# A hybrid decoder layer on one core: both matmuls of the MLP as 2x2 Strassen products, in two stages

## The chip, the core and the metric

The kernel runs on one core of a Trainium2 chip. The metric is the device time of one execution in microseconds; the time before is the median of three runs. Engine names follow the profile: PE (TensorE), DVE (VectorE), ACT (ScalarE), POOL (GpSimd), SP (SyncE, which issues nearly all transfers).

## What is computed

One layer over x of shape (1, 1024, 1024) float32. Three token mixers (an mLSTM, a short convolution, stick-breaking attention) come out of one input projection, are projected, gated and summed, and go through an output projection into the residual. The change touches only what follows:

```
x = x + merged @ w_out[l]                                   # 1024 x 1024
h2 = rmsnorm(x, norm_mlp_g[l])
x = x + jnp.square(jax.nn.relu(h2 @ w_up[l])) @ w_down[l]   # 1024 x 4096, 4096 x 1024
return rmsnorm(x, norm_final_g)
```

## The kernel before

**Arithmetic.** Each operand of a dense matmul is kept as two float32r tiles: `hi`, a copy made by ACT, and `lo`, the remainder made by DVE (`split`, lines 134 to 140). `mm3` (129 to 132) multiplies them with three matmuls: hi by hi, hi by lo, lo by hi. Every 128x128 by 128x512 product is thus three PE instructions.

**Storage.** Buffers lie in rings that are handed out and given back in program order: `ring_r` 64 tiles (names gr) of float32r operands, `ring_f` 23 float32 tiles (gf), `ring_wr` two raw weight tiles of 1056 columns (wr), `ring_wh` and `ring_wl` five each for the halves of a weight (wh, wl), and eight PSUM banks of 128x512 (ps). A buffer is written again only when its last reader is done.

**Order.** The program is traced in the order of the source; a scheduler then orders each engine's instructions by its own estimate of the times, and each engine runs its list in that order.

**Output projection and second norm** (740 to 808). For each of 8 tiles of 128 tokens, two groups of 24 matmuls make the product with `w_out`; DVE adds the residual (773), ACT squares with a sum (776), POOL takes the power -0.5 (204). After four tiles the normed tokens are multiplied by gain and factor (794), transposed on PE (800) and split straight from PSUM into `h2`, 8 x 2 pairs of 128x512.

**MLP** (810 to 848). Eight blocks F of 512 hidden columns. For each of 4 hidden tiles of a block, `dense_ws` (159) loads 1024x128 of `w_up`, splits it, and makes two groups of 24 matmuls, one per half of the tokens; ACT applies the Relu (822), DVE squares (823) and the result is split into `gT`. `load_rows` brings 128 rows of `w_down`. Then 16 groups of 12 matmuls (841) make the block's contribution for 8 token tiles by 2 halves of the columns, and DVE adds each to the residual `x1` (842), which stays in SBUF.

**End** (850 to 866). For each token tile two Squares, the factor, two multiplications (865) and two stores.

Of the kernel before, what the change touches and what calls it, by code (L numbers as in the profile page):

```python
# [38 lines left out]
def hybrid_block_kernel(  # L39
# [27 lines left out]
    # rings of equal buffers, handed out and given back in program order  # L67
# [74 lines left out]
    def load_split(src, k, parts):  # L142
        """Loads k rows of weights per partition and splits them into the (hi, lo) parts."""
# [557 lines left out]
    # branch projections under their gates  # L701
# [38 lines left out]
    # output projection, residual, second norm  # L740
# [12 lines left out]
    gb = [ring_f.get() for _ in range(2)]  # L753
    for c in range(2):
        nc.sync.dma_start(gb[c][:, :512], norm_mlp_g[:, c * 512:(c + 1) * 512].broadcast_to([P, 512]))
    x1 = [None] * 8
    rss = [None] * 8
    h2 = [[None, None] for _ in range(KO)]
    for th in range(2):
        for tl in range(4):  # L760
            tt = th * 4 + tl
            sl = slice(tl * P, (tl + 1) * P)
# [21 lines left out]
        if th == 1:
            for w2 in wo:
                free_all([w2])
        for ko in range(KO):
            h2[ko][th] = (g("mh"), g("mh"))
        for c in range(2):
            for t2 in range(2):  # L790
                xn = [ring_f.get(), ring_f.get()]
                for ti in range(2):
                    tt = th * 4 + t2 * 2 + ti
                    nc.vector.scalar_tensor_tensor(xn[ti][:, :512], x1[tt][c][:, :512], rss[tt], gb[c][:, :512], ALU.mult, ALU.mult)
# [99 lines left out]
```

## Time and profile before

| what | value |
|---|---|
| median of 3 runs | 2579.2 us (2579.11 to 2579.5) |
| span of the profiled execution | 2577.4 us, 1.8 us below that median |
| PE | busy 99% of the span, 13176 matmuls |
| DVE, ACT, POOL | busy 50%, 36%, 14% |
| granted PE clock | 0.999 of full speed |
| moved by DMA | 156.4 MB, 61 GB/s on average |

The profiled execution has no run time of its own beside its span; the span goes from its first to its last instruction. A matmul's "busy" time overlaps with the next one's, so the distance from one to the next is had by dividing a stretch by its matmuls, not from the mean of one. "Idle before" in a group is the time its engine sat idle just ahead of these instructions.

### The profile page before, as it was taken

What the parts mean: (1) busy time and instruction counts of PE and PEld (TensorE: products, weight loads), DVE (VectorE), ACT (ScalarE), POOL (GpSimd) and SP (SyncE); (2) the same over time, 40 slices, a digit from 0 to 9 for tenths busy, and PEclk for the clock granted to TensorE, in tenths of its full rate; (3) what the DMA queues carried; (4) which work ended last, traced back from release to release, by engine and by line L of the source; (5) the groups of instructions that cost most, each with busy time, mean ns of one, the idle gap of its engine ahead of it and who ended that gap; (6) DMA issues with size and microseconds to landing.
All of it is one profiled execution on the core that took longest, in us unless ns stands there. A gap on an engine that the chain in (4) does not pass through costs nothing.

```text
span 2577.4 us, 33885 instructions
## 1 busy us (share of the span) xinstructions
PE 2550.9 (99%) x13176; PEld 2155.3 (84%) x13176; DVE 1280.8 (50%) x2169; ACT 916.9 (36%) x1902; POOL 371.8 (14%) x840
## 2 busy tenths in 40 slices
PE   7999999999999999999999999999999999999998
PEld 6899898988888888888888888888888888888887
DVE  6465463667677577587422223234444333333434
ACT  6343343456455455455412213123222112211212
POOL 3000010044354254254100000000000000000000
PEclk9999999999999999999999999999999999999999
DMA  4121111212221211221312213223112101111211
GB/s 120 46 70 48 52 42 54 65 51 58 66 57 46 70 52 50 64 60 58 105 49 82 75 49 107 57 73 108 51 40 66 49 24 59 58 41 33 66 41 66
DMA packets 194248, 156.40 MB, mean 61 GB/s; under 512 B 12320, under 2 KB 172064, under 8 KB 194088
## 3 DMA queue, kind: packets, MB, share of 16 engines
q1 hardware_dynamic: 193944, 153.99, 20.6%
q8 instruction: 103, 1.69, 0.3%
q14 instruction: 57, 0.47, 0.1%
q10 hardware_dynamic: 144, 0.26, 0.0%
HBM read 129.04 MB, written 16.79 MB: 57 GB/s over the span
## 4 chain that ended last, share of the span: by engine, by line
PE 96%; DVE 2%; POOL 1%; issue 1%; DMA 0%; ACT 0%; SPq 0%; POOLq 0%; DVEq 0%; ACTq 0%
PE ps L130 29%; PE ps L131 29%; PE ps L132 29%; PE ps L590 2%; PE ps L557 1%; PE ps L556 1%; PE ps L607 1%; PE ps L606 1%; DVE gf L572 1%; POOL gf L573 0%; DMA wr<-in_w_in_dram 0%; PE ps L456 0%; PE ps L800 0%; POOL gf L564 0%; PE ps L603 0%
## 5 line engine op out<-in xcount | busy, mean ns | idle before, releaser
L131 PE MATMUL ps<-gr,wh 128*128 128x512 f32 x2176 | 860.6, 396 | 0.0
L130 PE MATMUL ps<-gr,wh 128*128 128x512 f32 x2176 | 860.4, 396 | 0.0
L132 PE MATMUL ps<-gr,wl 128*128 128x512 f32 x2176 | 860.2, 395 | 0.0
L132 PEld LDWEIGHTS ps<-gr,wl 128*128 128x128 f32 x2176 | 408.7, 188 | 94.2
L130 PEld LDWEIGHTS ps<-gr,wh 128*128 128x128 f32 x2176 | 409.0, 188 | 93.1
L131 PEld LDWEIGHTS ps<-gr,wh 128*128 128x128 f32 x2176 | 408.7, 188 | 93.0
L137 DVE TENSOR_TENSOR wl<-wr,wh 128x512 fp32r<-128x512 f32 (+1 forms) x320 | 226.1, 713 | 368.9 <-ACT wh L136 364.6
L136 ACT ACTIVATE wh<-wr 128x512 fp32r<-128x512 f32 (+1 forms) x320 | 200.2, 631 | 503.9 <-PE ps L131 383.0
L131 PE MATMUL ps<-gr,gr 128*128 128x512 f32 (+3 forms) x848 | 310.0, 367 | 0.0
L132 PE MATMUL ps<-gr,gr 128*128 128x512 f32 (+3 forms) x848 | 309.0, 366 | 0.0
L130 PE MATMUL ps<-gr,gr 128*128 128x512 f32 (+3 forms) x848 | 305.8, 365 | 0.0
L572 DVE TENSOR_TENSOR_SCAN gf<-gf 128x512 f32<-128x512 f32 (+1 forms) x192 | 201.1, 1049 | 99.8 <-POOL gf L564 56.3
L204 POOL TENSOR_TENSOR smalls<-smalls,mhalf 128x1 f32<-128x1 f32 (+1 forms) x40 | 26.2, 657 | 1419.7 <-DVE smalls L203 1419.6
L130 PE MATMUL ps<-wh,gr 128*128 128x256 f32 (+1 forms) x768 | 219.3, 286 | 2.6 <-ACT gr L139 2.6
L131 PE MATMUL ps<-wl,gr 128*128 128x256 f32 (+1 forms) x768 | 216.2, 282 | 0.0
L132 PE MATMUL ps<-wh,gr 128*128 128x256 f32 (+1 forms) x768 | 215.6, 284 | 0.2 <-DVE gr L140 0.2
L136 ACT ACTIVATE gr<-wr 128x512 fp32r<-128x512 f32 x128 | 75.8, 627 | 384.6 <-PE ps L132 293.7
L573 POOL TENSOR_TENSOR gf<-gf,gf 128x512 f32<-128x512 f32 (+1 forms) x192 | 185.3, 967 | 175.8 <-DVE gf L572 149.3
L136 ACT ACTIVATE gr<-ps 128x256 fp32r<-128x256 f32 (+2 forms) x336 | 141.4, 436 | 183.9 <-PE ps L132 70.5
L137 DVE TENSOR_TENSOR gr<-ps,gr 128x256 fp32r<-128x256 f32 (+2 forms) x336 | 155.7, 477 | 67.9 <-ACT gr L136 64.3
L842 DVE TENSOR_TENSOR gf<-gf,ps 128x512 f32<-128x512 f32 x128 | 87.8, 687 | 194.7 <-PE ps L132 194.7
L130 PEld LDWEIGHTS ps<-gr,gr 128*128 128x128 f32 x848 | 159.2, 188 | 29.1
(143 smaller groups left out, 2883.6 us busy)
## 6 DMA issues: line engine op xcount, KB each, us to landing
wr<-in_w_in_dram SPq DMA_DIRECT2D x102, 512.0 KB, 3.9
wr<-in_w_up_dram SPq DMA_DIRECT2D x32, 512.0 KB, 4.1
wr<-in_w_down_dram SPq DMA_DIRECT2D x32, 512.0 KB, 3.5
gr<-gr SPq DMA_DIRECT2D x64, 128.0 KB, 2.2
gf<-in_x_dram SPq DMA_DIRECT2D x31, 256.0 KB, 3.7
yml<-gf SPq DMA_DIRECT2D x32, 128.0 KB, 2.0
ysc<-gf SPq DMA_DIRECT2D x16, 256.0 KB, 2.0
ysb<-gf SPq DMA_DIRECT2D x32, 128.0 KB, 1.8
```

The lines of the kernel that those rows point to most:

```text
L130: mm(ps, lh, rh, start=start, stop=False)
L131: mm(ps, lh, rl, start=False, stop=False)
L132: mm(ps, ll, rh, start=False, stop=stop)
L136: nc.scalar.activation(hi, src, AF.Copy)
L137: nc.vector.tensor_tensor(lo, src, f32(hi), ALU.subtract)
L204: nc.gpsimd.tensor_tensor(dst, ms[:, :w], mhalf[:, :w], ALU.pow)
L556: mm(ps[:, :w], qs, kx[ch][:, :w], start=True, stop=False)
L557: mm(ps[:, :w], qs, ky[ch][:, :w], start=False, stop=True)
L572: nc.vector.tensor_tensor_scan(ur, ur, ur, u[:, w:w + 1], ALU.mult, ALU.bypass)
L573: nc.gpsimd.tensor_tensor(be[:, :w], be[:, :w], u[:, 1:w + 1], ALU.mult)
L590: nc.tensor.transpose(pt[:, k * 256 + ti * P:k * 256 + (ti + 1) * P], blk, ident)
L842: nc.vector.tensor_tensor(x1[tt][c][:, :512], x1[tt][c][:, :512], ps, ALU.add)
```

## The change

**Both products** become one level of Strassen in Winograd's form: operands are cut into 2x2 blocks, 7 block products take the place of 8, and sums of blocks are made on POOL (`pool_tt`), four for a left operand (`left`), four for a right one (`right`). The 7 products of a unit go into three PSUM banks (`BANK`, `FIRST`); several products follow one another in one bank, and the running sum is read out between them.

**Up.** A unit is 256 hidden columns by all 1024 tokens. Its left operand is `w_up` in four quarters of 128x512; its right operand, `hB`, is made once from the normed tokens: 7 sets of 4 pairs, in 56 of the 64 gr tiles. Each product is 12 matmuls. After the third, fourth and later products the running sums are copied (ACT), added (DVE), rectified (ACT) and squared (DVE) into four quarters of the hidden activations; `left` makes their four sums, and all seven left operands of the down product are written to DRAM (`gd`).

**Down.** A block is 512 hidden rows. `right` makes the sums of `w_down`, 14 pairs are split; each half of the block's work reads 7 left operands back from `gd`, splits them, and makes 7 x 2 products of 6 matmuls. Each running sum is added to the residual: four of seven by DVE out of PSUM, three by an ACT copy and a POOL add.

**Around them.** The residual `x1` is written to DRAM after the output projection and read back at the start of down. The gain of the second norm is now applied per partition by ACT when it evacuates the transposes, 64 of 128x128. The raw weight tiles serve as quarters, with 6 gf tiles more; wh, wl and the gr tiles left over form one ring (`wts`), to which the 56 tiles of `hB` are added for down.

```
-    def mm3(ps, lh, ll, rh, rl, start, stop):
+    def mm3(ps, lh, ll, rh, rl, start, stop, chain=False):
...
+    BANK = (0, 2, 0, 1, 0, 1, 0)
+    FIRST = (True, True, False, True, False, False, False)
...
+    def left(get, a11, a12, a21, a22):
+        s1, s2, s3, s4 = [get() for _ in range(4)]
+        pool_tt(s1, a21, a22, ALU.add)
+        pool_tt(s2, s1, a11, ALU.subtract)
+        pool_tt(s3, a11, a21, ALU.subtract)
+        pool_tt(s4, a12, s2, ALU.subtract)
+        return (a11, a12, s2, s1, s3, s4, a22), (s1, s2, s3, s4)
...
+                nc.sync.dma_start(x1_d[tt][:, c * 512:(c + 1) * 512], xt[:, :512])
...
+                for k in range(4):
+                    nc.tensor.transpose(ps[:, k * P:(k + 1) * P], xn[:, k * P:(k + 1) * P], ident)
+                for k in range(4):
+                    nc.scalar.activation(h2[th][c * 4 + k][:, sl], ps[:, k * P:(k + 1) * P], AF.Copy,
+                                         scale=gmlp[:, c * 4 + k:c * 4 + k + 1])
...
+    for k in range(4):
+        t2.append(ring_f.get())
+        pool_tt(t2[k], h2[1][4 + k], t1[k], ALU.subtract)
+        split(hB[2][k][0][:, :512], hB[2][k][1][:, :512], t2[k][:, :512])
...
+    for u in range(FF // 256):
...
+        parts, made = left(ring_f.get, a[0][0], a[0][1], a[1][0], a[1][1])
...
+        for i in range(7):
+            wh, wl = wts.get(), wts.get()
+            split(wh[:, :512], wl[:, :512], parts[i][:, :512])
...
+            for k in range(4):
+                ks = slice(k * P, (k + 1) * P)
+                rh, rl = hB[i][k]
+                mm3(ps, wh[:, ks], wl[:, ks], rh[:, :512], rl[:, :512], FIRST[i] and k == 0, k == 3, True)
+            free(wh, wl)
+            if i in (0, 2, 3):
+                s[i] = ring_f.get()
+                nc.scalar.activation(s[i][:, :512], ps, AF.Copy)
+            elif i == 1:
+                nc.vector.tensor_tensor(s[0][:, :512], s[0][:, :512], ps, ALU.add)
...
+        parts, made = left(ring_f.get, s[0], s[6], s[2], s[3])
+        for i in range(7):
+            nc.sync.dma_start(gd[u // 2][i][:, :, u % 2, :], parts[i][:, :512].rearrange("p (a c) -> p a c", a=2))
...
+    for j in range(FF // 512):
...
+            parts, made = right(ring_f.get, b[0][0], b[0][1], b[1][0], b[1][1])
+            for i in range(7):
+                hi, lo = wts.get(), wts.get()
+                split(hi[:, :512], lo[:, :512], parts[i][:, :512])
...
+        for tp in range(2):
+            gl = []
+            for i in range(7):
+                hi, lo = wts.get(), wts.get()
+                nc.sync.dma_start(f32(lo[:, :512]), gd[j][i][:, tp].rearrange("p k c -> p (k c)"))
+                nc.scalar.activation(hi[:, :512], f32(lo[:, :512]), AF.Copy)
+                nc.vector.tensor_tensor(lo[:, :512], f32(lo[:, :512]), f32(hi[:, :512]), ALU.subtract)
...
+            for i in range(7):
+                for t in range(2):
...
+                        mm3(ps, gl[i][0][:, o], gl[i][1][:, o], rh[:, :512], rl[:, :512], FIRST[i] and k == 0, k == 1, True)
...
+                    if i in (0, 3, 5):
+                        sn = ring_f.get()
+                        nc.scalar.activation(sn[:, :512], ps, AF.Copy)
+                        nc.gpsimd.tensor_tensor(acc, acc, sn[:, :512], ALU.add)
+                        free(sn)
+                    else:
+                        nc.vector.tensor_tensor(acc, acc, ps, ALU.add)
```

The order of instructions, at three places. First PE at the turn into the MLP, before: the last transposes (L800, out of two normed tiles) stand amid the first products of up.

```order
L130 MATMUL ps_165<-gr_69,wh_152 128x512
L800 MATMUL ps_162<-ident,gf_127 128x128
L800 MATMUL ps_162<-ident,gf_139 128x128
L800 MATMUL ps_162<-ident,gf_127 128x128
L800 MATMUL ps_162<-ident,gf_139 128x128
L131 MATMUL ps_167<-gr_70,wh_153 128x512
```

After the change PE ends the last transposes (L827) behind the first two products of the first unit, which need the first half of the tokens only, and goes on with the second unit's first product:

```order
L132 MATMUL ps_167<-gr_91,wh_155 128x512
L827 MATMUL ps_162<-ident,gf_144 128x128 x4
L827 MATMUL ps_163<-ident,gf_145 128x128 x4
L130 MATMUL ps_169<-gr_63,gr_89 128x512
L131 MATMUL ps_169<-gr_64,gr_89 128x512
L132 MATMUL ps_169<-gr_63,gr_90 128x512
```

DVE at the same place after the change: 27 rows from the first subtraction behind the last evacuated transposes to the `lo` half (wl_159) that the first unit's third product in PE's order needs; the last ten of them:

```order
L137 TENSOR_TENSOR gr_118<-gf_141,gr_117 128x512
L137 TENSOR_TENSOR gr_66<-gf_128,gr_65 128x512
L907 TENSOR_TENSOR gf_141<-gf_141,ps_167 128x512
L137 TENSOR_TENSOR gr_70<-gf_138,gr_69 128x512
L923 TENSOR_TENSOR gf_141<-gf_141 128x512
L137 TENSOR_TENSOR gr_74<-gf_132,gr_73 128x512
L137 TENSOR_TENSOR wl_161<-gf_135,wl_160 128x512
L137 TENSOR_TENSOR gr_78<-gf_143,gr_77 128x512
L907 TENSOR_TENSOR gf_129<-gf_129,ps_164 128x512
L137 TENSOR_TENSOR wl_159<-gf_144,wl_158 128x512
```

Splits of all right operands (gr) stand ahead of that weight; ACT has the same 27 in the same order, and 18 POOL sums come before it.

Second, DVE in the middle of down. Before, the additions out of PSUM (L842) come one after another:

```order
L842 TENSOR_TENSOR gf_135<-gf_135,ps_168 128x512
L842 TENSOR_TENSOR gf_136<-gf_136,ps_169 128x512
L842 TENSOR_TENSOR gf_145<-gf_145,ps_164 128x512
L842 TENSOR_TENSOR gf_149<-gf_149,ps_165 128x512
L842 TENSOR_TENSOR gf_133<-gf_133,ps_166 128x512
```

Now they (L985) alternate with subtractions for weights (L137) and for left operands (L964):

```order
L964 TENSOR_TENSOR wh_155<-wh_155,wh_154 128x512
L985 TENSOR_TENSOR gf_127<-gf_127,ps_162 128x512
L137 TENSOR_TENSOR gr_110<-gf_140,gr_109 128x512
L137 TENSOR_TENSOR gr_82<-gf_141,gr_81 128x512
L985 TENSOR_TENSOR gf_136<-gf_136,ps_163 128x512
L137 TENSOR_TENSOR gr_104<-wr_151,gr_103 128x512
L137 TENSOR_TENSOR gr_86<-wr_151,gr_85 128x512
L964 TENSOR_TENSOR gr_90<-gr_90,gr_89 128x512
```

A subtraction there stands behind additions that wait for PE, and an addition behind subtractions that wait for ACT.

Third, the end of DVE's list. Before, one pair of final multiplications (L865) is left behind the last addition:

```order
L842 TENSOR_TENSOR gf_144<-gf_144,ps_164 128x512
L842 TENSOR_TENSOR gf_131<-gf_131,ps_165 128x512
L861 TENSOR_TENSOR smalls<-smalls 128x1
L203 TENSOR_SCALAR smalls<-smalls 128x1
L865 SCALAR_TENSOR_TENSOR gf_144<-gf_144,smalls,gf_127 128x512
L865 SCALAR_TENSOR_TENSOR gf_131<-gf_131,smalls,gf_139 128x512
```

Now the last addition is followed by 14 of them (L1007), of which the first six are:

```order
L985 TENSOR_TENSOR gf_135<-gf_135,ps_163 128x512
L1007 SCALAR_TENSOR_TENSOR gf_149<-gf_149,smalls,gf_140 128x512
L1007 SCALAR_TENSOR_TENSOR gf_139<-gf_139,smalls,gf_141 128x512
L1003 TENSOR_TENSOR smalls<-smalls 128x1 x3
L203 TENSOR_SCALAR smalls<-smalls 128x1 x3
L1007 SCALAR_TENSOR_TENSOR gf_138<-gf_138,smalls,gf_140 128x512
L1007 SCALAR_TENSOR_TENSOR gf_137<-gf_137,smalls,gf_141 128x512
L1007 SCALAR_TENSOR_TENSOR gf_132<-gf_132,smalls,gf_140 128x512
L1007 SCALAR_TENSOR_TENSOR gf_134<-gf_134,smalls,gf_141 128x512
```

Seven token tiles' last multiplications moved behind the last addition.

## Rows read from the trace of the kernel before

**Rows 1.** The page: busy time of the engines, and PE's granted clock in 40 slices.
```profile
PE 2550.9 (99%) x13176; PEld 2155.3 (84%) x13176; DVE 1280.8 (50%) x2169; ACT 916.9 (36%) x1902; POOL 371.8 (14%) x840
...
PEclk9999999999999999999999999999999999999999
```

**Rows 2.** The page: the chain that ended last, by engine.
```profile
PE 96%; DVE 2%; POOL 1%; issue 1%; DMA 0%; ACT 0%; SPq 0%; POOLq 0%; DVEq 0%; ACTq 0%
```

**Rows 3.** Windows, 1900 to 2500 us: length, busy us of each engine, clock, DMA.
```profile
1900.00:2500.00 600.00, 600.00 (x2586) 485.50 (x2586) 219.91 (x326) 128.66 (x215) 0.00 (x0) 1.00 0.15 47
```

**Rows 4.** Groups by shape, 1600 to 2577 us: count, busy us, mean ns, idle before.
```profile
L130 PE MATMUL ps<-gr,wh 128*128 128x512 f32 x743 | 292.7, 396 | 0.0
...
L842 DVE TENSOR_TENSOR gf<-gf,ps 128x512 f32<-128x512 f32 x128 | 87.8, 687 | 194.7 <-PE ps L132 194.7
L137 DVE TENSOR_TENSOR wl<-wr,wh 128x512 fp32r<-128x512 f32 x90 | 61.9, 691 | 128.0 <-ACT wh L136 128.0
L136 ACT ACTIVATE wh<-wr 128x512 fp32r<-128x512 f32 x90 | 56.3, 630 | 157.6 <-PE ps L131 92.5 <-DMA wr<-in_w_up_dram 56.3 <-PE ps L800 4.7
...
L823 DVE TENSOR_TENSOR gf<-gf 128x512 f32<-128x512 f32 x64 | 44.3, 692 | 97.4 <-ACT gf L822 97.1
L822 ACT ACTIVATE gf<-ps 128x512 f32<-128x512 f32 x64 | 38.2, 598 | 105.5 <-PE ps L132 105.5
...
L865 DVE SCALAR_TENSOR_TENSOR gf<-gf,smalls,gf 128x512 f32<-128x512 f32 x16 | 11.3, 749 | 5.2 <-POOL smalls L204 5.2
...
L800 PE MATMUL ps<-ident,gf 128*128 128x128 f32 x64 | 9.1, 272 | 0.0
```

**Rows 5.** Groups by shape, the whole run.
```profile
L573 POOL TENSOR_TENSOR gf<-gf,gf 128x512 f32<-128x512 f32 x96 | 117.0, 1218 | 111.6 <-DVE gf L572 90.0 <-ACT gf L613 5.7 <-ACT gr L136 4.5
...
L136 ACT ACTIVATE gr<-ps 128x128 fp32r<-128x128 f32 x64 | 18.0, 282 | 36.3 <-DVE gr L137 35.5
```

**Rows 6.** Timeline at 637 us: start us, duration us, instruction, idle before; DVE, then POOL.
```profile
637.06 0.67 DVE L639 TENSOR_TENSOR gf<-gf,ps 128x512 f32<-128x512 f32 x1
637.64 1.29 DVE L137 TENSOR_TENSOR wl<-wr,wh 128x512 fp32r<-128x512 f32 x1
...
637.29 1.09 POOL L573 TENSOR_TENSOR gf<-gf,gf 128x512 f32<-128x512 f32 x1 [1.40 <-DVE gf L572]
```

**Rows 7.** Timeline at 630 us, DVE, then POOL.
```profile
630.52 0.73 DVE L642 SCALAR_TENSOR_TENSOR gf<-gf,cw,gf 128x512 f32<-128x512 f32 x1
631.29 1.47 DVE L643 SCALAR_TENSOR_TENSOR gf<-gf,cw,gf 128x512 f32<-128x512 f32 x1
...
630.75 1.45 POOL L573 TENSOR_TENSOR gf<-gf,gf 128x512 f32<-128x512 f32 x1 [1.31 <-DVE gf L572]
```

**Rows 8.** Windows at the kernel's start.
```profile
20.00:24.00 4.00, 1.66 (x13) 1.42 (x12) 2.77 (x10) 1.92 (x6) 4.00 (x4) 1.00 0.98 247
24.00:28.00 4.00, 3.58 (x17) 2.83 (x18) 3.97 (x11) 1.72 (x5) 4.00 (x4) 0.67 0.07 18
28.00:32.00 4.00, 4.00 (x32) 3.95 (x32) 1.68 (x5) 1.51 (x5) 2.18 (x2) 0.90 0.02 4
40.00:48.00 8.00, 6.18 (x44) 4.94 (x42) 6.37 (x14) 4.17 (x7) 0.53 (x1) 1.00 0.01 2
8.00:16.00 8.00, 4.66 (x20) 3.75 (x21) 7.16 (x21) 6.11 (x15) 3.73 (x5) 1.00 1.06 386
```

**Rows 9.** Timeline of the end.
```profile
2568.02 0.39 PE L130 MATMUL ps<-gr,gr 128*128 128x512 f32 x1
...
2568.25 0.40 PE L131 MATMUL ps<-gr,gr 128*128 128x512 f32 x1
...
2570.31 0.69 DVE L842 TENSOR_TENSOR gf<-gf,ps 128x512 f32<-128x512 f32 x1 [1.02 <-PE ps L132]
...
2571.85 0.16 DVE L861 TENSOR_TENSOR smalls<-smalls 128x1 f32<-128x1 f32 x1 [0.85 <-ACT gf L858]
...
2572.86 1.42 DVE L865 SCALAR_TENSOR_TENSOR gf<-gf,smalls,gf 128x512 f32<-128x512 f32 x2 [0.66 <-POOL smalls L204]
```

**Rows 10.** DMA issues: size of each, median us from issue to landing.
```profile
wr<-in_w_up_dram SPq DMA_DIRECT2D x32, 512.0 KB, 4.1
wr<-in_w_down_dram SPq DMA_DIRECT2D x32, 512.0 KB, 3.5
```

More of the change, by code (lines that the diff above doesn't have):

```diff
@@ L752, in hybrid_block_kernel @@
     wo.append(load_rows(w_out, D - P))
[L753 to L758, printed above, removed]
+    h2 = [[None] * KO for _ in range(2)]
+    hB = [None] * 7
     for th in range(2):
+        for ko in range(KO):
+            h2[th][ko] = ring_f.get()
         for tl in range(4):
@@ L782, in hybrid_block_kernel @@
+            free(*x1)
         for ko in range(KO):
             free(*mhl[ko][th])
[L784 to L788, printed above, removed]
[L789 to L807 removed]
@@ new lines, in hybrid_block_kernel @@
+        if th == 0:
+            for i in (0, 1):
+                hB[i] = [(g("mh"), g("mh")) for _ in range(4)]
+                for k in range(4):
+                    split(hB[i][k][0][:, :512], hB[i][k][1][:, :512], h2[0][i * 4 + k][:, :512])
+    for w2 in wo:
+        free_all([w2])
+    unplan(ring_r, "wd")
+    unplan(ring_r, "mh")
+    for i in range(2, 7):
+        hB[i] = [(ring_r.get(), ring_r.get()) for _ in range(4)]
+    t1, t2 = [], []
+    for k in range(4):
+        t1.append(ring_f.get())
+        pool_tt(t1[k], h2[1][k], h2[0][k], ALU.subtract)
+        free(h2[0][k])
@@ new lines, in hybrid_block_kernel @@
+    for k in range(4):
+        t2.append(ring_f.get())
+        pool_tt(t2[k], h2[1][4 + k], t1[k], ALU.subtract)
+        split(hB[2][k][0][:, :512], hB[2][k][1][:, :512], t2[k][:, :512])
+    for k in range(4):
+        split(hB[3][k][0][:, :512], hB[3][k][1][:, :512], t1[k][:, :512])
+        free(t1[k])
+    for k in range(4):
+        t3 = h2[1][k]
+        pool_tt(t3, h2[1][4 + k], t3, ALU.subtract)
+        split(hB[4][k][0][:, :512], hB[4][k][1][:, :512], t3[:, :512])
+        free(t3)
@@ new lines, in hybrid_block_kernel @@
+    for k in range(4):
+        split(hB[5][k][0][:, :512], hB[5][k][1][:, :512], h2[1][4 + k][:, :512])
+        free(h2[1][4 + k])
+    for k in range(4):
+        t4 = h2[0][4 + k]
+        pool_tt(t4, t4, t2[k], ALU.subtract)
+        split(hB[6][k][0][:, :512], hB[6][k][1][:, :512], t4[:, :512])
+        free(t4, t2[k])
+    unplan(banks, "acc", "tp")
+    plan(banks, p=8)
+    quarters = Ring([t[:, o:o + 512] for t in ring_wr.tiles for o in (0, 528)], "q")
+    own_q = move(ring_f, quarters, 6)
```

158 lines of the change are left out of this document (101 added, 57 removed).

## The prediction

> **What bounds the kernel now.** I read the page's engine line first, then the chain that ended last, then the MLP's own stretch in windows, and only then groups of instructions. The page shows TensorE (PE) busy 99% of the span at full granted clock in every slice [rows 1], and the chain is 96% PE [rows 2]. In the MLP the window from 1900 to 2500 us has PE busy for all 600 us, with 2586 matmuls, so one matmul costs 600 / 2586 = 0.232 us there (starts in the last stretch of the trace lie 0.23 apart [rows 9]); VectorE (DVE) is busy 220 of those 600 us, ScalarE (ACT) 129, GpSimd (POOL) 0 [rows 3]. So time goes down only if PE gets fewer matmuls, and each us in which PE then waits for another engine comes straight back. The view of waits has no wait of PE there; the PE rows of the groups have an idle time of 0.0 [rows 4]. Today the other engines are loosely loaded. The change loads them heavily, so most of the working is about whether they keep up. Times below are against the profiled span of 2577.4 us; the median of the runs, 2579.2, lies 1.8 above it, and I add that at the end.
>
> **What is removed.** Before, up is 32 x 2 x 8 x 3 = 1536 matmuls and down 8 x 16 x 4 x 3 = 1536. After, up is 16 units x 7 products x 12 = 1344, and down 8 blocks x 2 halves x 7 x 2 x 6 = 1344. That is 384 fewer: 384 x 0.232 = **-89.1 us**. The 64 transposes stay in number. One unit of up is now 84 matmuls, 19.5 us of PE; one block of down 168, 39.0 us.
>
> **The steady up stage.** Per unit DVE gets 7 subtractions of splits, 3 additions from PSUM and 4 squares, 14 x 0.69 = 9.7 us [rows 4]; ACT 7 halves of splits, 4 evacuations and 3 Relus, 14 x 0.63 at most = 8.8; POOL 8 sums of 128x512. A POOL add of that shape takes 1.09 us when nothing disturbs it [rows 6] and 1.22 on average [rows 5], so 8.7 to 9.8 us. All three are near half of 19.5 us. Two units are interleaved in the new order of PE, and the ring of weight buffers has 9 pairs, so splits can run ahead. I price this at +3; the bounds are 0 and one POOL add per unit, 16 x 1.09 = 17, since a late sum is what a split would wait for.
>
> **The steady down stage.** Per block DVE gets 14 splits of weights, 14 of left operands and 16 additions from PSUM: 44 x 0.69 = 30.4 us. ACT gets 28 x 0.63 + 12 x 0.60 = 24.8. POOL gets 8 + 12 adds, 20 x 1.09 = 21.8. Against 39.0 us of PE each fits by itself. But DVE and POOL disturb each other: at 637.29 POOL begins an add; the DVE addition with one input in PSUM beside it takes its usual 0.67, while the DVE subtraction of two SBUF tiles that follows takes 1.29 instead of 0.69, so it lost 0.60 [rows 6]. At 630.75 a POOL add takes 1.45, and a DVE instruction of two SBUF tiles behind it takes 1.47 where its twin took 0.73, a loss of 0.74 [rows 7]. So a POOL add costs DVE between 0 (it meets a PSUM addition, or idle time) and 0.74: DVE needs 30.4 to 45.2 us per block, and PE 39.0. That bounds the stage at +0 to 8 x 6.2 = +50. I take 0.35 for a mean POOL add, half of 0.74, because 16 of the 44 DVE instructions read PSUM and DVE has some idle time: 37.4 us, which is 96% of PE's time. Queues so full, served in a fixed order, wait for each other; I put 2 us per block on that, **+16**.
>
> The Trainium skill ("SBUF — State Buffer", Who interferes with whom) says that DVE and GpSimd share a port pair under an exclusive lock held for the whole instruction. The trace agrees that the two exclude each other, but a subtraction lost 0.60 to 0.74, not the 1.09 of a whole add. By the rule, taken to its end, the stage would cost what the first rival below gives.
>
> **The turn into the MLP.** Before, PE passes it without a wait (the transposes and the products beside them have an idle time of 0.0 [rows 4]). Now five of the seven right operands need the second half of the tokens, four of them as sums on POOL, so they begin when the last transposes are evacuated. From the last matmul of the output projection, PE has two products (24 matmuls, 5.6 us) that cover the norm chain, the last 8 transposes (at most 8 x 0.27 = 2.2 [rows 4]) and two more products, 13.3 us in all. The fifth product needs a split that stands 27th on ACT and 27th on DVE behind the last evacuations, as the order of the change shows. Those evacuations, 8 of 0.28 [rows 5] beside the transposes, end near 9 us; 27 x 0.69 = 18.6 on DVE brings 27.6. PE so idles at least 14 us. Eighteen POOL adds stand before that split too; each may cost DVE 0.60, +11, and if all 27 rows are disturbed +16. Bounds +14 and +30. I take 22, the middle, since POOL works through that whole time. Idle time of that length also costs clock: at the kernel's start, PE busy 1.66 of 4 us is followed by windows at 0.67 and 0.90 of the clock (both mix its two levels, 2.4 and 1.2 GHz), a loss of 4 x 0.33 + 4 x 0.10 = 1.7 us, while 6.18 of 8 us busy kept it at 1.00 [rows 8]. With 2 for that: **+24**.
>
> **The turn from up to down.** DVE has 8 rows between the second-last product's sum and the first split of the new stage, 5.5 us against one product of 2.8 us, and 9 more until both halves of the first right operands stand. 17 x 0.69 = 11.7, less 2.8 and less 2.8 of PE work that is ready: bounds +3 and, with 17 x 0.60 of disturbance, +16. **+8**.
>
> **The end.** Before, one norm is left when PE ends: DVE's last sum at 2570.31, its last instruction done at 2574.28, span's end 2577.4, 7.1 us [rows 9]. Now DVE's queue has 14 of the final multiplications [rows 4] and 12 small ones [rows 9] behind its last sum, 14 x 0.75 + 12 x 0.16 = 12.4, with 0.7 and 3.1 around them: 16.2. **+9** (6 to 11).
>
> **What costs nothing.** Passing the left operands adds 112 writes and 112 reads of 256 KB, 29.4 MB each way, and x1 4.2 each way. Up then moves 16.8 + 29.4 MB in 312 us, 148 GB/s, as does down. The stretch of 1900 to 2500 has 47 GB/s at a DMA share of 0.15 [rows 3], so this is a share near 0.47; the kernel's start has 386 GB/s [rows 8]. Landings of 3.5 to 4.1 us [rows 10] are covered as long as the loads are issued a product or two ahead; without that cover the third rival's price holds. SP's queue gets some 18 issues per 39 us. The first norm's Square, the 64 evacuations of 128x128 and the x1 copies lie beside 89 us of output projection.
>
> **Sum:** -89.1 + 3 + 16 + 24 + 8 + 9 = -29. Span 2548, time **2550 us**.
>
> **The rivals.**
> 1. *DVE and POOL take turns entirely* (slower). If each POOL add costs DVE its whole 1.09, a block of down takes 30.4 + 21.8 = 52.2 us, 13.2 over PE: +106 in place of +16, 2640 us. For it: 28 of DVE's 44 instructions there read two SBUF tiles, and POOL is busy for more than half of the time. Against it: the losses seen are 0.60 and 0.74 [rows 6, 7]. It decides where the stage costs 45 in place of 16 us: 5.6 a block, DVE at 44.6, so from 0.71 for each of the 20 adds. The lock that the Trainium skill describes, named above, would be its cause. Chance 0.20.
> 2. *The cover holds.* Only the first turn's lower bound and the end stay: -89.1 + 14 + 9 = -66, 2513 us. For it: every engine has less than 80% of work of its own. Chance 0.15.
> 3. *One queue for all transfers.* SP issues writes that wait for POOL and the loads behind them in order; if each of the 16 halves of down waits for one landing of 3.5 us, +56, 2606 us; from 1.8 us a half it is slower than before. Against: left operands of all blocks but the last lie in DRAM long before. Chance 0.08.
> 4. *Fewer matmuls, but slower ones.* Groups of 6 alternate between banks where 12 or 24 ran on; at 0.265 us instead of 0.232 the gain is gone. Nothing in the trace shows such a price. Chance 0.03.
>
> **How the numbers follow.** My forecast, stalls in part, has 0.54 and by its bounds 2528 to 2576. About 0.2% (5 us) is what a measurement of this kernel can tell from none. Faster: nearly all of the forecast, all of rival 2 and a little of rival 1 where it stays weak, 0.71; within 0.2%: the edges, 0.08; slower: most of rivals 1, 3 and 4, 0.21. The range that leaves out about 0.2 reaches from rival 2 to rival 3: 2510 to 2604.
>
> **What would show it.** Right: PE's count down by 384; windows of PE full in the middle of up, and over 90% in down; a gap of 14 to 30 us of PE before the second half of the first up unit, with a dip of the clock; DVE above 90% in down with subtractions of 128x512 above 0.69 on average; the end after the last matmul some 16 us long. Wrong: PE full at both turns (rival 2); DVE without idle time and PE below 80% in down (rival 1); PE's waits ended by DMA tiles (rival 3); a pitch above 0.232 where PE never waits (rival 4).

## The result, and the profile after

The changed kernel takes 2601.0 us (median of 4 runs, 2599.9 to 2601.9), against 2579.2 before: ratio 1.0086, with a 95% interval from 1.0071 to 1.0100. It is slower, by 0.9%. The prediction of 2550 us had the wrong sign; the time lies just inside its range, near the upper end.

The page of the changed kernel, answering to [rows 1, 2]: engines, clock, and the chain by engine.

```profile
PE 2490.0 (96%) x12792; PEld 2087.6 (80%) x12792; DVE 1552.8 (60%) x2357; ACT 1092.2 (42%) x2250; POOL 841.5 (32%) x1144
...
PEclk9999999999999999999999999999889999899999
...
PE 4%; POOL 3%; issue 3%; DVE 3%; DMA 2%; ACT 1%; SPq 0%; DVEq 0%; POOLq 0%; ACTq 0%
```

PE has 384 matmuls fewer, as intended. The chain could be followed back from the end only to 2187 us, so its shares add up to 16% and do not compare with the 96% of before; in that stretch no engine leads. The windows of the stages (turn into the MLP, up, turn from up to down, down; columns as in [rows 3]):

```profile
1860.00:1910.00 50.00, 19.68 (x61) 14.04 (x60) 42.65 (x33) 21.31 (x42) 39.36 (x24) 0.66 0.26 75
1950.00:2150.00 200.00, 196.67 (x839) 156.56 (x839) 131.87 (x139) 80.00 (x139) 117.24 (x79) 1.00 0.45 144
2200.00:2250.00 50.00, 34.59 (x121) 25.79 (x120) 31.27 (x38) 24.31 (x43) 25.40 (x17) 0.80 0.73 245
2300.00:2500.00 200.00, 186.01 (x767) 143.87 (x766) 176.55 (x201) 100.37 (x182) 142.87 (x90) 0.98 0.40 136
```

PE is full in none of them. In the first, DVE is busy 42.65 of 50 us with only 33 instructions, POOL 39.36 with 24: each is occupied, and slow.

A loss per stage is worked out here, for every kernel below too, from the starts of the matmuls: the length of a stage less 0.232 us for each matmul in it (0.1 for a transpose). The stages run from the output projection's last matmul over the first 252 PE instructions of up; on to the 84th matmul before down; from there over down's first 84; and to the last matmul. The tail is what follows that, to the span's end.

| us lost | turn into MLP | up | turn to down | down | tail |
|---|---|---|---|---|---|
| forecast | 24 | 3 | 8 | 16 | 16.2 |
| the change | 37.4 | 7.3 | 22.7 | 35.5 | 16.1 |

Losses of 102.9 and 8.8 more of tail than the 7.3 that the kernel before has by the same measure, less the 89.1 saved, make +22.6; the span grew by 21.3, so 1.3 us are unassigned.

Where the time of the other engines goes shows in the groups by shape of the stretch 2255 to 2575 us, down (columns as in [rows 4]):

```profile
L982 POOL TENSOR_TENSOR gf<-gf,gf 128x512 f32<-128x512 f32 x89 | 141.0, 1602 | 89.6 <-ACT gf L981 89.1 <-DVE gr L137 0.6
...
L964 DVE TENSOR_TENSOR gr<-gr,gr 128x512 fp32r<-128x512 f32 x83 | 93.5, 1145 | 6.7 <-ACT gr L963 6.7
L985 DVE TENSOR_TENSOR gf<-gf,ps 128x512 f32<-128x512 f32 x122 | 80.5, 676 | 7.0 <-PE ps L132 5.8 <-POOL gf L982 1.2
...
L137 DVE TENSOR_TENSOR gr<-gf,gr 128x512 fp32r<-128x512 f32 x51 | 56.1, 1101 | 19.0 <-ACT gr L136 17.4
...
L759 POOL TENSOR_TENSOR gf<-wr,gf 128x512 f32<-128x512 f32 x28 | 46.3, 1655 | 0.9
L137 DVE TENSOR_TENSOR gr<-wr,gr 128x512 fp32r<-128x512 f32 x36 | 33.8, 960 | 5.8 <-ACT gr L136 5.8
...
L759 POOL TENSOR_TENSOR gf<-wr 128x512 f32<-128x512 f32 x14 | 22.6, 1615 | 0.7
L759 POOL TENSOR_TENSOR gf<-wr,wr 128x512 f32<-128x512 f32 x14 | 21.6, 1541 | 0.4
```

DVE's additions with one input in PSUM (L985) take 676 ns, no more than the 687 of before [rows 4]. Its subtractions of two SBUF tiles take 960 to 1145 ns in place of 691. POOL's sums take 1541 to 1655, where I counted 1090. Who waited for whom in that stretch (us in total, times, longest):

```profile
ACT gr L136 <- POOL gf L759: 90.5, 43, 4.1
POOL gf L982 <- ACT gf L981: 89.1, 31, 7.6
...
PEld ps L130 <- DVE gf L985: 23.5, 20, 2.8
...
PE ps L130 <- DVE gf L985: 15.2, 15, 2.3
```

PE waits for banks that DVE has not yet added up, and ACT for sums that POOL has not yet made. Of transfers PE waits for none here. Of the 35.5 us lost in down, 8.3 are no waits: 64 of PE's matmuls start some 0.36 us apart, at half clock or changing to it.

The end, answering to [rows 9], has DVE's last sum and, behind it, final multiplications (x counts them):

```profile
2582.83 0.69 DVE L985 TENSOR_TENSOR gf<-gf,ps 128x512 f32<-128x512 f32 x1 [0.45 <-PE ps L132]
...
2585.78 2.74 DVE L1007 SCALAR_TENSOR_TENSOR gf<-gf,smalls,gf 128x512 f32<-128x512 f32 x4 [0.54 <-POOL smalls L204]
...
2590.77 4.06 DVE L1007 SCALAR_TENSOR_TENSOR gf<-gf,smalls,gf 128x512 f32<-128x512 f32 x6 [0.54 <-POOL smalls L204]
```

With four more ahead and between, these are the 14 multiplications of the forecast.

The clearest place is the turn into the MLP. The timeline from 1866.6 us (start, length, instruction):

```profile
1866.60 11.80 DVE L137 TENSOR_TENSOR gr<-gf,gr 128x512 fp32r<-128x512 f32 x7
1867.76 11.81 POOL L759 TENSOR_TENSOR gf<-gf,gf 128x512 f32<-128x512 f32 x7
```

Both engines run seven instructions in the same 11.8 us: 1.69 us for one of each. PE's waits between 1855 and 1915 us:

```profile
PE ps L130 <- ACT wl L136: 13.6, 1, 13.6
PE ps L132 <- DVE gr L137: 7.7, 2, 7.5
PE ps L130 <- ACT gr L136: 6.2, 1, 6.2
PE ps L132 <- DVE wl L137: 2.9, 1, 2.9
```

These are 30.4 of the 37.4 us; the rest is mostly half clock, as the 0.66 of the window above shows, a mix of the levels 1.2 and 2.4 GHz behind these waits.

The turn from up to down looks different: from 2209.8 to 2223.9 us POOL stands idle, waiting for the last unit's squares. What follows is one chain, from the view of the chain that ended last (start, length, engine and what it makes):

```profile
2223.92 2.27 POOL gf L759
...
2227.47 3.48 DMA gd<-gf
...
2231.09 1.27 POOL gf L759
...
2232.38 0.63 ACT gr L136
...
2233.04 5.47 DMA wr<-in_w_down_dram
...
2238.53 0.64 ACT wh L136
...
2239.21 2.07 PE ps L130 x4
```

POOL makes the last unit's sums, they are written to DRAM (`gd`), and only behind such a write POOL makes its next sum of `right`. That sum is split; a load of `w_down` starts only now and is split in turn. PE waits 6.2 us for the first of these splits and 2.8 for the second. POOL's queue is not what holds it here, and two links of the chain are transfers.

### The profile page after: what moved, and what is told of

Read it like the earlier page. It is cut to its first block, busy times and chain, and to the rows that moved or that the text cites. A ratio compares the mean times of both kernels' runs of the same rounds, so it can differ in the third digit from the quotient of the medians.

```text
span 2598.7 us, 35067 instructions
## 1 busy us (share of the span) xinstructions
PE 2490.0 (96%) x12792; PEld 2087.6 (80%) x12792; DVE 1552.8 (60%) x2357; ACT 1092.2 (42%) x2250; POOL 841.5 (32%) x1144
## 5 line engine op out<-in xcount | busy, mean ns | idle before, releaser
L132 PE MATMUL ps<-gr,wl 128*128 128x512 f32 x1854 | 735.0, 397 | 2.9 <-DVE wl L137 2.9
L130 PE MATMUL ps<-gr,wh 128*128 128x512 f32 x1844 | 730.8, 396 | 4.2 <-DVE gf L985 1.7
L131 PE MATMUL ps<-gr,wh 128*128 128x512 f32 x1844 | 729.5, 396 | 0.0
L132 PEld LDWEIGHTS ps<-gr,wl 128*128 128x128 f32 x1854 | 349.4, 188 | 83.4 <-DVE wl L137 3.6
L130 PEld LDWEIGHTS ps<-gr,wh 128*128 128x128 f32 x1844 | 346.9, 188 | 85.0 <-DVE gf L910 2.9
L131 PEld LDWEIGHTS ps<-gr,wh 128*128 128x128 f32 x1844 | 346.7, 188 | 78.3
L137 DVE TENSOR_TENSOR wl<-wr,wh 128x512 fp32r<-128x512 f32 (+1 forms) x260 | 186.0, 722 | 297.9 <-ACT wh L136 293.5
L204 POOL TENSOR_TENSOR smalls<-smalls,mhalf 128x1 f32<-128x1 f32 (+1 forms) x40 | 26.5, 667 | 716.1 <-DVE smalls L203 716.0
L573 POOL TENSOR_TENSOR gf<-gf,gf 128x512 f32<-128x512 f32 (+1 forms) x192 | 185.4, 968 | 176.4 <-DVE gf L572 145.2
L130 PE MATMUL ps<-wh,gr 128*128 128x256 f32 (+2 forms) x800 | 232.4, 292 | 8.9 <-DVE gf L985 3.3
L137 DVE TENSOR_TENSOR gr<-gf,gr 128x512 fp32r<-128x512 f32 (+2 forms) x186 | 182.3, 994 | 93.0 <-ACT gr L136 89.6
L131 PE MATMUL ps<-wl,gr 128*128 128x256 f32 (+2 forms) x804 | 231.3, 288 | 0.0
L132 PE MATMUL ps<-wh,gr 128*128 128x256 f32 (+2 forms) x800 | 228.6, 289 | 0.2 <-DVE gr L140 0.2
L759 POOL TENSOR_TENSOR gf<-gf,gf 128x512 f32<-128x512 f32 x111 | 169.4, 1547 | 125.1 <-DVE gf L923 104.4
L136 ACT ACTIVATE gr<-gf 128x512 fp32r<-128x512 f32 (+2 forms) x186 | 113.5, 625 | 192.6 <-POOL gf L759 159.2
```

The lines of the kernel that those rows point to most:

```text
L130: mm(ps, lh, rh, start=start, stop=False, skip_group_check=chain)
L131: mm(ps, lh, rl, start=False, stop=False, skip_group_check=chain)
L132: mm(ps, ll, rh, start=False, stop=stop, skip_group_check=chain)
L136: nc.scalar.activation(hi, src, AF.Copy)
L137: nc.vector.tensor_tensor(lo, src, f32(hi), ALU.subtract)
L204: nc.gpsimd.tensor_tensor(dst, ms[:, :w], mhalf[:, :w], ALU.pow)
```

## The experiments

**Theory A**: a POOL sum and a DVE instruction with two SBUF inputs exclude each other; both pay. **Theory B**: the sums are merely late, and everything stands behind them in fixed order. **Theory C**: the transfers through DRAM and the half clock make the losses. All ratios are to the kernel before. The scheduler orders each of these kernels anew, so two of them differ in some rows of the lists beside the edit.

| kernel | us | ratio (95%) | turn in | up | turn to down | down | tail |
|---|---|---|---|---|---|---|---|
| the change | 2601.0 | 1.0086 (1.0071 to 1.0100) | 37.4 | 7.3 | 22.7 | 35.5 | 16.1 |
| 1 no sums | 2502.2 | 0.9703 (0.9688 to 0.9717) | 5.4 | 0.1 | 4.3 | -0.3 | 11.9 |
| 2 dead sums | 2563.3 | 0.9936 (0.9921 to 0.9951) | 27.1 | 0.0 | 24.2 | 13.3 | 15.0 |
| 3 up's right sums on DVE | 2588.8 | 1.0038 (1.0026 to 1.0051) | 26.5 | 5.0 | 23.1 | 36.7 | 16.1 |
| 4 all on DVE | 2539.7 | 0.9847 (0.9833 to 0.9862) | 21.3 | 0.0 | 17.5 | 6.9 | 11.3 |
| 5 `left` on DVE | 2578.6 | 0.9999 (0.9990 to 1.0008) | 27.8 | 0.0 | 16.2 | 36.4 | 16.1 |
| 6 running sums on DVE | 2573.2 | 0.9976 (0.9967 to 0.9985) | 36.0 | 7.6 | 23.9 | 11.7 | 11.7 |
| 7 as 4, turn reordered | 2543.5 | 0.9866 (0.9850 to 0.9882) | 24.1 | 0.2 | 17.6 | 7.1 | 10.7 |
| 8 as 7, and two more | 2543.9 | 0.9863 (0.9848 to 0.9878) | 24.8 | 0.2 | 12.1 | 15.8 | 9.5 |
| 9 as 4, residual late | 2541.5 | 0.9856 (0.9839 to 0.9872) | 21.3 | 0.0 | 11.2 | 14.0 | 11.6 |
| 10 as 9, turn by need | 2546.7 | 0.9876 (0.9861 to 0.9891) | 25.9 | 0.2 | 10.9 | 16.8 | 11.6 |
| 11 as 4, halves split in up | 2558.5 | 0.9923 (0.9906 to 0.9940) | 28.2 | 0.4 | 35.2 | 2.0 | 11.0 |
| 12 as 11, residual late | 2543.8 | 0.9864 (0.9850 to 0.9879) | 27.7 | 0.4 | 23.4 | -0.3 | 11.0 |

### 1. No sums

```
-        return (a11, a12, s2, s1, s3, s4, a22), (s1, s2, s3, s4)
+        return (a11, a12, a21, a22, a11, a12, a22), ()
...
-                        nc.gpsimd.tensor_tensor(acc, acc, sn[:, :512], ALU.add)
```

> All sums of POOL in the MLP are left out: `left`, `right` and the right operands of up hand on raw blocks in place of sums, and the three copied running sums per token pair in down are not added, so the output is not the layer's. All splits, products, evacuations and transfers stay. Theory A (a POOL sum and a DVE instruction with two SBUF tiles exclude each other, so DVE pays some 0.9 us per sum): DVE needs 44 x 0.69 = 30.4 us per block of 39.0, the turn into the MLP falls to its lower bound of some 14 to 18 us, the turn from up to down to about 5, steady up to 2, steady down to 5 to 10, the end stays at +9: about 2530 us, some 70 below the change. Theory B (the sums come late and everything stands behind them in fixed order, whatever DVE pays): the same fall here, 2525 to 2545. Theory C (the losses are of the transfers through DRAM and of half clock after the turns): 2585 or more.

Measured 2502.2 us, 28 below A's 2530 and 23 below the range of B. The turn, up and down windows:

```profile
1860.00:1910.00 50.00, 47.08 (x198) 36.92 (x197) 31.27 (x51) 28.89 (x57) 0.00 (x0) 0.97 0.48 147
1950.00:2150.00 200.00, 200.00 (x864) 161.95 (x863) 92.06 (x141) 84.47 (x143) 0.00 (x0) 1.00 0.49 153
...
2300.00:2450.00 150.00, 150.00 (x649) 121.59 (x648) 103.49 (x166) 84.23 (x147) 0.00 (x0) 1.00 0.44 140
```

PE is full with the same transfers, splits and evacuations as in the change, so the 99 us between the two come from the sums. C falls as a cause by itself: at 140 to 153 GB/s the transfers cost PE nothing in up and down, and the turn from up to down, with all its transfers, loses 4.3 us.

### 2. Dead sums

```
-        return (a11, a12, s2, s1, s3, s4, a22), (s1, s2, s3, s4)
+        return (a11, a12, a21, a22, a11, a12, a22), (s1, s2, s3, s4)
...
-                        nc.gpsimd.tensor_tensor(acc, acc, sn[:, :512], ALU.add)
+                        nc.gpsimd.tensor_tensor(sn[:, :512], sn[:, :512], sn[:, :512], ALU.add)
```

> As the kernel without sums, but POOL makes every sum at its old place into scratch, and nothing reads the results: the products work on raw blocks. No instruction of DVE, ACT or PE waits for the result of a sum (a buffer comes free later at most). Theory A: the time comes back nearly to that of the change, 2585 to 2601 us, with DVE subtractions of 1.0 to 1.6 us where POOL works beside them. Theory B: within 10 us of the kernel without sums.

Measured 2563.3 us, outside the ranges of both A and B: sums that nobody reads cost 61.0 us, and reading them 37.8 more. The timeline at the turn, DVE, then POOL:

```profile
1869.41 25.81 DVE L137 TENSOR_TENSOR gr<-gf,gr 128x512 fp32r<-128x512 f32 x16 [0.86 <-ACT gr L136]
...
1881.44 11.79 POOL L759 TENSOR_TENSOR gf<-gf,gf 128x512 f32<-128x512 f32 x7
```

and the groups of 2240 to 2540 us:

```profile
L979 POOL TENSOR_TENSOR gf<-gf 128x512 f32<-128x512 f32 x89 | 115.8, 1311 | 95.8 <-ACT gf L978 95.8
L961 DVE TENSOR_TENSOR gr<-gr,gr 128x512 fp32r<-128x512 f32 x84 | 92.3, 1116 | 4.4 <-ACT gr L960 4.0
L982 DVE TENSOR_TENSOR gf<-gf,ps 128x512 f32<-128x512 f32 x123 | 80.6, 675 | 14.1 <-PE ps L132 14.0
L137 DVE TENSOR_TENSOR gr<-wr,gr 128x512 fp32r<-128x512 f32 x82 | 75.2, 962 | 21.5 <-ACT gr L136 21.4
```

The subtractions (1.61 us each at the turn, 0.962 and 1.116 in down) are about as slow as in the change although nothing waits for a result of POOL; those with a PSUM input keep 0.675. That is A's mark. Presence alone makes most of the loss at the first turn (27.1 of 37.4) and all of it at the second (24.2); but there it works through buffers: PE's one wait of 14.1 us is for a split whose load of `w_down` starts late, since POOL reads the tiles late. In down presence makes 13.3 of 35.5. The other 22 are not all waits for results: the dead running sums read one tile twice and take 1.31 us, where those of the change take 1.60, so this run presses less on DVE; and 6 of the 22 are half clock (8.3 us in the change, 2.3 here). That results come late above all because DVE slows POOL is argued from POOL's 1.60 us a sum, not shown apart.

### 3. The right sums of up on DVE

```
-        pool_tt(t1[k], h2[1][k], h2[0][k], ALU.subtract)
+        dve_tt(t1[k], h2[1][k], h2[0][k], ALU.subtract)
```

and so for the other twelve.

> The 16 sums for the right operands of up (once, at the turn into the MLP) go from POOL to DVE; all else stays. Theory A: in place of pairs of a sum and a subtraction that take some 3.2 us where both pay 1.6, DVE does a pair in 1.4; 43 instructions of 0.69 are 29.7 us, plus 9 before them, less 13.3 of cover, plus 2 for the clock: a turn of 27 in place of 37, so about 2591 us. Theory B: 16 more instructions stand ahead on the queue that PE waits for, +11: 2605 to 2612 us.

Measured 2588.8 us, as A said (2591), against 2605 or more by B alone. Sixteen more instructions on the queue that PE waits for shorten that turn by 10.9 us.

### 4. All sums on DVE

```
     def left(get, a11, a12, a21, a22):
-        pool_tt(s1, a21, a22, ALU.add)
+        dve_tt(s1, a21, a22, ALU.add)
...
-                    if i in (0, 3, 5):
-                        sn = ring_f.get()
-                        nc.scalar.activation(sn[:, :512], ps, AF.Copy)
-                        nc.gpsimd.tensor_tensor(acc, acc, sn[:, :512], ALU.add)
-                        free(sn)
-                    else:
-                        nc.vector.tensor_tensor(acc, acc, ps, ALU.add)
+                    nc.vector.tensor_tensor(acc, acc, ps, ALU.add)
```

> All sums of the MLP go from POOL to DVE, and the three running sums per token pair that ACT copied and POOL added are added by DVE straight from PSUM (the ACT copies fall away). DVE has 22 x 0.69 = 15.2 us per up unit of 19.5 and 64 x 0.69 = 44.2 us per down block of 39.0, so it is over PE in down by 5.2 a block, 42 us. Theory A: the up stage loses under 5, the first turn 27, the second about 12, the end 9: about 2588 us, a little faster than the change although DVE has 45% more to do. Theory B: DVE's longer queue costs more everywhere: 2615 or more.

Measured 2539.7 us: 61.4 below the change, 39.5 below the kernel before (ratio 0.9847). No kernel of this study that computes the layer is faster. It is also 48 below A's 2588: I had expected down to lose 42 us at 64 x 0.69 = 44.2 of DVE a block; it lost 6.9. Windows of up and down, a timeline row of DVE, and two groups of 2235 to 2520 us:

```profile
1950.00:2150.00 200.00, 200.00 (x864) 161.93 (x863) 147.75 (x231) 87.22 (x146) 0.00 (x0) 1.00 0.45 145
...
2300.00:2450.00 150.00, 146.25 (x628) 117.41 (x627) 149.16 (x249) 64.85 (x110) 0.00 (x0) 1.00 0.47 153
```

```profile
1862.27 6.11 DVE L762 TENSOR_TENSOR gf<-gf,gf 128x512 f32<-128x512 f32 x10 [3.06 <-ACT gf L832]
```

```profile
L982 DVE TENSOR_TENSOR gf<-gf,ps 128x512 f32<-128x512 f32 x203 | 134.0, 679 | 9.1 <-PE ps L132 9.0
...
L762 DVE TENSOR_TENSOR gf<-wr,gf 128x512 f32<-128x512 f32 x27 | 18.4, 682 | 0.0
```

DVE is busy 149.16 of 150 us with 249 instructions, one per 0.60 us; ten in a row take 6.11. The mean of one in a group, 0.68, counts an overlap of 0.08 twice. At 0.60 a block needs 38.4 us of DVE, under PE's 39.0. (The pitch could be read before: two starts at 637.06 and 637.64 [rows 6].)

The turn from up to down still loses 17.5 us, though nothing collides there any more. PE's two longest waits at that turn are those of the change, for the first splits of down's weights:

```profile
2202.85 1.22 PE L130 MATMUL ps<-gr,gr 128*128 128x512 f32 x2 [6.73 <-ACT gr L136]
...
2210.05 2.08 PE L130 MATMUL ps<-wh,gr 128*128 128x512 f32 x4 [4.26 <-ACT wh L136]
```

### 5 and 6. One group of sums at a time

Run 5 moves `left` alone (diff as in 4), run 6 only the running sums (the second hunk of 4).

> Only the sums of `left` (8 for each unit of up) go from POOL to DVE; those for the right operands of up, of `right` and the running sums in down stay on POOL. Theory A (POOL and DVE exclude each other): the steady up stage, which lost 7.3 us, loses under 1; the two turns, in which 8 to 16 of these sums fall, lose 3 to 8 less; down keeps its 35: 2586 to 2592 us. Theory B (order and late sums): DVE's longer queue undoes it, 2598 or more.

> Only the three running sums per token pair that ACT copied and POOL added (12 a block) go to DVE straight from PSUM; `right` stays on POOL. DVE instructions with an input in PSUM took 0.68 us beside POOL sums in every run so far. Theory A: 12 of the 20 POOL sums of a block are gone and DVE gets 12 cheap instructions; the down stage loses some 15 in place of 35.5, so about 2580 us. A rival within A, that `right`'s sums alone make the loss because the weight splits stand behind them: 2592 or more.

Run 5 took 2578.6 us, more gained than A said: up lost nothing more, the turns 9.6 and 6.5 less. Run 6 took 2573.2: down lost 11.7 in place of 35.5, and the tail fell from 16.1 to 11.7, though `right` still ran on POOL. So the rival that `right` alone makes the loss falls. Runs 3, 5 and 6 gain 12.3, 22.4 and 27.9 us, each mainly in the stages where it takes sums from POOL. Together that is 62.6, and run 4, which moves `right` as well, gains 61.4: moving `right` too gained nothing more, if the gains add up.

### 7 to 10. Order alone

Run 7 writes the first two products of units 0 and 1 ahead of up's right sums. Run 8 adds the residual's loads behind the first block's, and the last half block token tile by token tile. Run 9 is run 4 with the residual's move alone. Run 10 adds to run 9 the turn in the order of need. In short:

```
+    early = []
+    for u in range(2):
...
+        for i in range(2):
+            product(i, q4[0][i], bank, s)
...
+        if j == 0:
+            x1 = [[ring_f.get(), ring_f.get()] for _ in range(8)]
```

> The kernel with all sums on DVE, and the first two products of units 0 and 1, which need the first half of the tokens only, are written ahead of the sums for the right operands, with their weights in the four tile pairs that are free during the output projection. PE then has four products (11.1 us) behind the output projection in place of two before it needs a sum. If the turn is set by what PE has ready while DVE and ACT make the right operands, its loss falls from 21.3 to 8 to 14 us: 2526 to 2533 us. If it is set by DVE's throughput over the whole turn, whatever the order, it stays: 2537 or more.

> As the one before, and two more changes of order: the residual is read back behind the first block's loads in down in place of ahead of them, and in the last half of the last block each token tile gets all its seven products in turn, with its final norm written right behind it. If the turn from up to down waits for transfers queued behind the 4.2 MB of the residual, its loss falls from 17.5 to some 10 us; the end falls from 11.3 to some 8: 2516 to 2524 us. If that turn is set by splits in the queues of ACT and DVE, only the end changes: 2524 to 2530 us.

> The kernel with all sums on DVE, with one move: the residual is read back behind the first block's loads in down in place of ahead of them. The run with three changes of order lost 12.1 us at the turn from up to down in place of 17.5, and lost 8.9 more in down, which I put down to its token tiles' own order in the last block. If that is right: 2534 us (2532 to 2537). If the residual's place costs down what the turn gains: 2539.

> As the one before, and the turn into the MLP is written in the order in which PE needs things: four products that need the first token half only, then the sums and splits of right operands 2 and 3, then unit 0's own sums and its weights for these two products, and only then the other sums and splits. In the run with the plain reordering PE sat 20.8 us in one wait for a weight that stood behind all right operands on the queues of ACT and DVE. Here 8 + 4 + 4 + 4 + 4 + 1 = 25 DVE instructions stand between the last evacuated transposes and that weight, 15 us at the 0.60 at which DVE issued back to back, against 6 us of products left by then: a wait of 9 and, with the clock, a loss of 11 in place of 21 to 24: 2522 to 2526 us. If the turn is set by DVE's throughput over the whole of it: 2534.

All four missed the gain that I forecast: 2543.5, 2543.9, 2541.5 and 2546.7 us, none below run 4, whose own runs reach 2541.4. Run 7 came out on the side of its second branch, DVE's throughput (2537 or more), and run 9 near its second (2539). In run 7 PE's several waits became one, and in run 10 too. The wait in each, and in run 10 what DVE did ahead of it:

```profile
1888.61 0.79 PE L130 MATMUL ps<-gr,wh 128*128 128x512 f32 x1 [20.78 <-ACT wh L136]
```

```profile
1867.21 7.31 DVE L762 TENSOR_TENSOR gf<-gf,gf 128x512 f32<-128x512 f32 x12 [0.77 <-ACT gf L832]
...
1889.66 0.80 PE L130 MATMUL ps<-gr,gr 128*128 128x512 f32 x1 [18.95 <-ACT gr L136]
```

In both orders of the source the scheduler put twelve sums on DVE in a row, and the splits that PE needs behind them; DVE also began its sums later than in run 4, by 2 us in run 7 and 5 in run 10; that this is because PE ran more products ahead of the last transposes is argued. At the other turn, moving the residual gained 6.3 us (run 9) and down gave back 7.1. The sum of the two stages is 24.4 in run 4, 25.1 in run 9, 27.7 in run 10: DVE has the same work to do from there to the end, which runs 11 and 12 test. I had put run 8's loss in down to its token order; run 9, without that order, has most of it, so that was wrong.

### 11 and 12. Splits moved from down into up

```
+            nc.scalar.activation(hi[:, :512], lo, AF.Copy)
+            nc.vector.tensor_tensor(lo.bitcast(F32R), lo, f32(hi[:, :512]), ALU.subtract)
+            nc.sync.dma_start(gd[u // 2][i][:, :, u % 2, :], f32(hi[:, :512]).rearrange("p (a c) -> p a c", a=2))
+            nc.sync.dma_start(gdl[u // 2][i][:, :, u % 2, :], lo.rearrange("p (a c) -> p a c", a=2))
```

> The kernel with all sums on DVE, and the left operands of down are split in up, where DVE has room, and go through DRAM as two halves. In the last two runs what the turn from up to down gained was lost again in down: turn and down together lost 24.4, 25.1 and 27.7 us. If DVE's total work from the end of up on is what bounds it (64 instructions a block, 38.6 us at 0.60, against 39.0 of PE), then with 50 a block, 30 us, down loses under 2 and the turn about 12; up has 29 x 0.60 = 17.5 us of DVE per 19.5 and loses 0 to 5. About 2528 us (2522 to 2533). If transfers are the limit there, doubling those of the left operands to some 240 GB/s costs more than it gains: 2545 or more, with PE's waits ended by transfers.

> As the one before, with the residual read back behind the first block's loads. With DVE no longer full in down, what the turn gains stays: 5 us under the one before, about 2523 us. If DVE is not what gave it back, the same as the one before within 2 us.

The part on down came true: with 50 DVE instructions a block it lost 2.0 and -0.3 us, so DVE was its bound in run 4. (ACT has 14 instructions a block fewer too, but was busy only 64.85 of 150 us in run 4.) The total did not: 2558.5 and 2543.8, for the turn from up to down lost 35.2 and 23.4, and the first turn 28.2 and 27.7 in place of 21.3. PE's and ACT's waits at that turn, run 11, then run 12:

```profile
PE ps L130 <- DMA gr<-gd: 8.7, 1, 8.7
```

```profile
PE ps L130 <- ACT wl L136: 12.1, 1, 12.1
...
ACT wl L136 <- DMA gd<-wl: 7.6, 1, 7.6
```

Here transfers do count: a split waits for a tile that is still being written to DRAM, and a product for one being read. Theory C, which does not explain the change, holds for this turn of the variant.

## Why the prediction was wrong

**Right.** The 384 matmuls and their 0.232 us; the tail (16.1 for 16.2); transfers hidden in the steady stages; the four places of loss. Rival 4 did not occur. Rival 3, late loads behind writes that wait for POOL, did not occur in down, but is part of the chain at the turn from up to down. That the time lies inside the range at all is luck: its upper end, 2604, was taken from rival 3's price in down (2606), which did not come.

**The step that failed: the price of a POOL sum beside a DVE subtraction.** I took 0.35 us of DVE per sum in down and at most 0.60 at the first turn, from single meetings in [rows 6, 7], in which POOL was partly done when DVE came, and I took POOL's own duration as the undisturbed one. A second term, that of the turn from up to down, left out a whole chain. By places:

- *At the first turn* the engines have queues full of such work. A pair takes 1.69 us where DVE alone issues at 0.60: each sum costs DVE 1.09 us, not 0.60. The loss was 13.4 us beyond my term. A second flaw: I counted four products as cover, but the third needs a weight half that stands eighth among the subtractions, so PE waited 6.2 and 7.5 us around its start. My upper bound of 32 fell.
- *At the turn from up to down* the loss was 14.7 us beyond my term of 8, which counted 17 rows of DVE and put nothing on the wait of these rows for POOL's sums, for the write to DRAM and for the loads. The price of a collision is the smaller part there: with all sums on DVE the turn still lost 17.5 of the 22.7 us (run 4), without sums 4.3 (run 1). On run 4's kernel, reading the residual back later, which also takes its 16 tiles later, brought it to 11.2 (run 9), so the order of loads and tiles is part of it; on the change itself that was not run.
- *What DVE does to POOL* was not in the sum at all. The 145 sums in the groups above (three L759 forms and L982) took 231.5 us, 1.60 each, so 32 of a block's 39 us in place of 21.8. A subtraction or addition of L759 with no such DVE instruction beside it took 1.25 to 1.31 us in 27 cases; my 1.09 was that of a multiplication [rows 5, 6].
- *In down* DVE lost on average (1145 - 691) x 83 + (1101 - 691) x 51 + (960 - 691) x 36 = 68 us over those 145 sums (the 36 are subtractions out of wr), 0.47 a sum. That is no great error. But with POOL at 1.6 the halves made from its sums come late, and PE's banks wait behind them in DVE's list. Dead sums, which cost DVE (1116 - 691) x 84 + (962 - 691) x 82 = 58 us by the same count and let nothing wait for their results, lost 13.3, near my 16; the change lost 35.5. The 2 us a block that I put on queues that wait for each other should have been some 2.4 more.

Together, with 4.3 more in up than forecast (a loss that is gone in run 5, with `left` on DVE): 13.4 + 4.3 + 14.7 + 19.5 = 52 us, against the 51 between 2550 and 2601.

**Rival 1** had the right mechanism and the wrong place. Nearly full turn-taking shows where both queues are full, at the first turn. In down, additions out of PSUM do not take part, and the mean price was 0.47, under the 0.71 that I named as the deciding point for that stage alone; the change was slower all the same, through late sums in down and through the two turns. The Trainium skill ("SBUF — State Buffer", Who interferes with whom) says that a DVE instruction with two SBUF inputs contends with a GpSimd instruction that reads SBUF, for a shared port pair under an exclusive lock, and that one with at most one SBUF input, outside its 2-port modes, does not. The traces agree with both halves: 1.69 us a pair, and 0.675 to 0.680 for PSUM additions in down in every run with sums on POOL there. They also show a limit: the pair takes 0.2 us less than the two alone, 1.29 + 0.60 = 1.89. I had set my 0.60 to 0.74 against that rule; but for those 0.2, the measurement decides for the rule.

**Why moving work onto the busier engine helps.** At the first turn the reason is DVE's own time: a sum on POOL costs it 1.09 us when both queues are full, the same sum on DVE 0.60. In down it is not, for 0.47 is less than 0.60: run 4 gives DVE about 300 instructions more, and DVE is busy 1567.7 us in its page, against 1552.8 in the change's. What goes away in down is the wait for POOL, whose sums took 1.60 us each; run 6 removes 12 of a block's 20 and has most of that gain (11.7 us lost in place of 35.5; run 4, 6.9). That the waits alone make this gain is argued, since these runs also end the collisions.

Not settled: how far better order could bring down the first turn's 21 us in run 4. The runs that tried it were undone by the scheduler's list.

## What to carry to other kernels

Before work is given to POOL as a helper of DVE, look at how many SBUF tiles DVE's instructions beside it read: with two, the two engines take turns, and where both queues are full the help costs DVE more than doing the work itself (1.09 us against 0.60 here). Read the price of a collision where both queues are full, and charge it to both engines; a single meeting in a quiet trace shows a part of it. Where one stage hands over to the next, follow the chain from the last result through sums, writes and loads to the first product, besides counting rows. And take an engine's capacity from the distance between starts, not from the mean length of its records.

## What was unexpected of the hardware

- A pair of POOL subtraction and DVE subtraction, 128x512 float32, all in SBUF, takes 1.69 us; DVE alone does two in 1.20.
- DVE starts back-to-back 128x512 instructions 0.60 us apart, though each record is 0.68 long.
- POOL with no such DVE instruction beside it: 1.29 us (median) for an add or subtraction of two 128x512 tiles, 1.09 for a multiplication (L573), 1.04 for an add that reads one tile twice (run 2).
- PE at half clock after the waits at the turn: in the change 0.66 of the clock over 50 us, in run 1, with hardly a wait there, 0.97.
